# Opening stretch and latents of a two-layer hybrid trunk emitted in hand order, its relative bias on quarters of the PE array

## The chip, the cores and the metric

One core of one Trainium2 chip runs the whole program in one launch. Its engines are TensorE (PE, matmuls; PEld is its weight load), VectorE (DVE), ScalarE (ACT), GpSimd (POOL) and SyncE (SP, which here issues nearly all DMAs). Each takes its instructions from its own queue in order. The metric is device time in microseconds (us), lower is better; a measurement here is the median of several runs, and one more execution is profiled.

## The reference, cut to what matters

Two layers, each with a modulated norm, one wide input projection, three branches (differential attention with a relative position bias, latent attention, a state-space branch), gates, and a feed-forward part; sequence 512, width 1024, all float32. The part that the change touches is the start of layer 0 and the bias, which both layers use:

```python
c_act = jax.nn.silu(c)
mod = c_act @ ada_w[l] + ada_b[l]               # [6 * 1024], here chunks 0 to 3 of 12
sh_m, sc_m, g_m, sh_f, sc_f, g_f = jnp.split(mod[:, None, :], 6, axis=-1)
h = _rmsnorm(x, norm_mix[l]) * (1 + sc_m) + sh_m
proj = h @ w_in[l]                              # the latents are 416 + 16 of its columns
...
dist = qpos[:, :, None] - positions[:, None, :]
bias = jnp.take(rel_table, _t5_bucket(dist), axis=0)   # 32 buckets, 4 heads
```

## The kernel before, in words

Activations are kept as features by tokens: eight tiles of 128 x 512. Matmuls in reduced float32 are made exact enough by splitting each operand into a high and a low part and adding three products (`mm3`, lines 145 to 147). `split` (line 131) makes the parts of a weight: an ACT copy writes `wh`, a DVE subtraction writes `wl`; three buffers of each rotate, each at an offset of some 64-byte lines. A planner orders each engine's queue by its own estimate of when things are ready, except where `tc.manual_schedule` fixes emission order for the engines that it names, or `keep_in_program_order` pins an instruction behind its engine's last one.

The opening prepares layer 0. `conditioning` makes `c_act`. `mod_steps` (line 498 on) loads four chunks of `ada_w` in 512 KB pieces (`wm`, eight buffers) and multiplies them into `macc` on DVE, two multiplies a piece (lines 520 and 522); its last step transposes `macc` on PE and sums it into `mod` (lines 529 to 535). `load_x` (line 485), `transpose_x` (lines 491 and 492) and `norm_r` (line 678; the root by POOL's pow on line 110, spread over partitions on line 685) prepare x. `norm_tiles` (lines 698 to 702) makes, for each half of the tokens and each of eight tiles, `tmp` on DVE, `hh` on ACT and `hl` on DVE.

The relative bias comes in 16 groups (4 blocks of 128 queries, 4 groups of 32 queries in each). A group covers 4 heads by 32 queries, 128 output rows, by the keys that a block sees (128 to 512). Eight steps each compare the key positions with the start of every bucket for 4 queries: `pk <= pq`, as a Sign on ACT (line 653, five of eight), a comparison on DVE (line 655, two) or on POOL (line 649, one). Each comparison tile is then multiplied by a table of bucket differences, high and low part, into all 128 rows of one PSUM bank, 16 matmuls (line 666). The bank is copied to `ob` and written by a POOL DMA to `bias_d` in DRAM, from where the attention reads it much later (line 1294). `START` is the order in which these parts are emitted: L loads x, V loads vectors, T transposes a tile of x, N is a step of the norm, S a step of the modulation, G a bias group.

Then come all norm tiles, `vectors` and `rotary` (small parameters, and sines), and the latents: `latent_product` (line 273 on) multiplies 8 tiles by 432 columns in two halves of 8 steps, 6 matmuls each (lines 299 to 301). After them `mix` begins the state-space branch with `lin_feat` (lines 145 to 147).

Of the kernel before, what the change touches and what calls it, by code (L numbers as in the profile page):

```python
# [9 lines left out]
F32 = mybir.dt.float32  # L10
# [8 lines left out]
P = 128  # L19
# [24 lines left out]
START = "LSSSTGTVNGSNNGSNSGGSGSTTSGTSGSGSGNGGSGTSGSGSGTT"  # L44
# [21 lines left out]
def trunk_kernel(ctx: ExitStack, tc: tile.TileContext, a: dict, out: bass.AP):  # L66
# [206 lines left out]
    def latent_product(l, pool, hh, hl):  # L273
# [12 lines left out]
        def prep():  # L286
            return [group(g) for g in range(3)]
# [210 lines left out]
    def mod_steps(l, j, pool=None):  # L498
# [4 lines left out]
        def step(s):  # L503
            if s == 0:
                acc.append(pool.tile([P, 512], F32, name="macc", bufs=4) if pool else sm.tile([P, 512], F32, name="macc", bufs=2))
# [7 lines left out]
            def pin(ins):  # L513
                tc.keep_in_program_order(ins)
# [11 lines left out]
        def total():  # L526
            mp = mbank()
            for q in range(4):
                ins = nc.tensor.transpose(out=mp[:, q * P:(q + 1) * P], in_=acc[0][:, q * P:(q + 1) * P], identity=ident)
                if pool:  # L530
                    tc.keep_in_program_order(ins)
# [6 lines left out]
        if not pool:  # L538
            return todo + [total]

        def last(s=KT // width - 1):
            step(s)
            total()
        return todo[:-1] + [last]
# [33 lines left out]
    bias_d = dram.tile([DA_H, P, BLK[T]], F32, name="bias_d")  # L578
# [3 lines left out]
    NSIGN = 5  # L582
    early, ahead, SLOW, DEEP = [], [0], (6,), 1
    ORDER = (7, 4, 0, 5, 1, 2, 3, 6)

    W = 2 * P + QG

    def rel_tables(bp):

        pk_i = bp.tile([P, S], I32, name="pk_i")  # L590
        nc.sync.dma_start(out=pk_i, in_=a["positions"].broadcast_to([P, S]))
        tab = bp.tile([P, DA_H], F32, name="tab")
        nc.sync.dma_start(out=tab, in_=a["rel_bias"].unsqueeze(0).broadcast_to([QG, BUCKETS, DA_H]))
        zero = bp.tile([P, 1], F32, name="zero")
        nc.vector.memset(zero, 0.0)
        lr = bp.tile([P, NJ * W], F32R, name="lr")
        nc.scalar.activation(lr, zero.broadcast_to([P, NJ * W]), AF.Copy)

        diff = bp.tile([P, P], F32, name="diff")
        nc.vector.tensor_tensor(out=diff[:, 1:P], in0=ident[:, 1:P], in1=ident[:, 0:P - 1], op=ALU.subtract)  # L600
        nc.vector.tensor_copy(out=diff[:, 0:P:BUCKETS], in_=ident[:, 0:P:BUCKETS])
        hdiff = bp.tile([P, P], F32, name="hdiff")
# [3 lines left out]
        st_row = bp.tile([1, QG, BUCKETS], F32, name="st_row")  # L606
# [4 lines left out]
        start = bp.tile([P, 1], F32, name="start")  # L611
# [15 lines left out]
        delta = bp.tile([P, 2, 2, DA_H], F32R, name="delta")  # L627
        nc.vector.tensor_copy(out=delta[:, :, 0], in_=dv)
        nc.vector.tensor_tensor(out=delta[:, :, 1], in0=dv, in1=delta[:, :, 0], op=ALU.subtract)
        lwv = lr.rearrange("p (j w) -> p j w", w=W)[:, :, 0:2 * P].rearrange("p j (x h q) -> p j x h q", x=2, h=DA_H)  # L630
        for i in range(QG):
            pr = slice(i * BUCKETS, (i + 1) * BUCKETS)
            for kind, js in ((0, slice(0, NSIGN)), (1, slice(NSIGN, NJ))):
                n = js.stop - js.start
                nc.vector.tensor_copy(out=lwv[pr, js, :, :, i],
                                      in_=delta[pr, kind].unsqueeze(1).broadcast_to([BUCKETS, n, 2, DA_H]))
        return pk, pq, pqh, lr[:, 0:NJ * 2 * P].rearrange("p (j x m) -> p j x m", j=NJ, x=2)

    def rel_bias(bp, tables, t, g):

        pk, pq, pqh, lr = tables
        nq = NJ * QG
        n = (t + 1) * P

        def step(t, g, j):
            c, w = (t * 4 + g) * NJ + j, t * P + (P if j == NJ - 1 else g * nq + (j + 1) * QG)
            if j in SLOW:
                st = bp.tile([P, S], F32R, name="sp", bufs=DEEP * len(SLOW) + 1)
                nc.gpsimd.tensor_scalar(out=st[:, 0:w], in0=pk[:, 0:w], scalar1=pq[:, c:c + 1], scalar2=None, op0=ALU.is_le)
            else:  # L650
                st = bp.tile([P, S], F32R, name="st", bufs=7)
                if j < NSIGN:
                    nc.scalar.activation(st[:, 0:w], pk[:, 0:w], AF.Sign, bias=pqh[:, c:c + 1], scale=-1.0)
                else:
                    nc.vector.tensor_scalar(out=st[:, 0:w], in0=pk[:, 0:w], scalar1=pq[:, c:c + 1],
                                            scalar2=None, op0=ALU.is_le)
            return st[:, 0:w]
        bank = mbank()
        while ahead[0] < min(4 * T, 4 * t + g + 1 + DEEP):
            early.append({j: step(ahead[0] // 4, ahead[0] % 4, j) for j in SLOW})  # L660
            ahead[0] += 1
        slow = early.pop(0)
        for j in ORDER:
            st = slow[j] if j in SLOW else step(t, g, j)
            for x in range(2):
                nc.tensor.matmul(bank[:, 0:st.shape[1]], lr[:, j, x], st, start=j == NJ - 1 and x == 0,  # L666
                                 stop=j == ORDER[-1] and x == 1)
        ob = bp.tile([P, S], F32, name="ob", bufs=3)
        nc.any.tensor_copy(out=ob[:, 0:n], in_=bank[:, 0:n])
        nc.gpsimd.dma_start(out=bias_d[:, g * nq:(g + 1) * nq, BLK[t]:BLK[t + 1]], in_=ob[:, 0:n])  # L670


    def norm_r(np_, x_tok):

        ss = small([P, T], "xss", 1)
        for t in range(T):
            sq = np_.tile([P, D], F32, name="sq")
            ins = nc.scalar.activation(sq, x_tok[:, t], AF.Square, accum_out=ss[:, t:t + 1])
            if t == 0:
                tc.keep_in_program_order(ins)  # L680
# [65 lines left out]
    def mix(l, x, hh, hl, ckr, cq, latp, scope):  # L746
# [258 lines left out]
        with ExitStack() as att:  # L1005
# [282 lines left out]
            def da_unit(h, t):  # L1288
# [3 lines left out]
                def scores():  # L1292
                    bt = dap.tile([P, S], F32, name="bt", bufs=3)
                    nc.sync.dma_start(out=bt[:, 0:n], in_=bias_d[h, :, BLK[t]:BLK[t + 1]])
# [200 lines left out]
    norm_scope = ExitStack()  # L1495
    np_ = norm_scope.enter_context(tc.tile_pool(name="norm0", bufs=1, reuse_waits="tile"))
    ip = norm_scope.enter_context(tc.tile_pool(name="init", bufs=1, reuse_waits="tile"))
    bp = norm_scope.enter_context(tc.tile_pool(name="bias", bufs=1, reuse_waits="tile"))
    conditioning(np_)
    tables = rel_tables(bp)  # L1500
    first = [f for j in (0, 2, 1, 3) for f in (mod_steps_pe if j in ON_PE else mod_steps)(0, j, ip)]
    x_tok = ip.tile([P, T, D], F32, name="x_tok")
    xT = big.tile([P, KT, S], F32, name="x16")
    groups = [(t, g) for t in range(T) for g in range(BUCKETS // NJ)]
    turn, rows = transpose_x(x_tok, xT), norm_r(np_, x_tok)
    for what in START:
        if what == "L":
            load_x(x_tok)
        elif what == "V":
            mod_vectors(0, np_)  # L1510
        elif what == "T":
            next(turn)
        elif what == "N":
            rb = next(rows)
        elif what == "S":
            first.pop(0)()
        else:
            rel_bias(bp, tables, *groups.pop(0))
    hh, hl = h_tiles()
    s1 = norm_scale(0, V_NMIX, 8)  # L1520
    for h in range(2):
        norm_tiles(np_, xT, 0, s1, 0, rb, hh, hl, HALF[h], range(KT))
    vectors(0, np_)
    rotary(np_)
    norm_scope.close()
    keep = ctx.enter_context(tc.tile_pool(name="keep", bufs=1, reuse_waits="tile"))
    latp = ctx.enter_context(tc.tile_pool(name="lat", bufs=1, side="right", reuse_waits="tile"))
    ckr = keep.tile([P, T, 176], F32, name="ckr")
    cqs = []
    with tc.tile_pool(name="wx", bufs=1, reuse_waits="tile") as pool:  # L1530
        run_halves(latent_product(0, pool, hh, hl))
# [56 lines left out]
```

## Time and profile before

| | us |
|---|---|
| median of 3 runs (2073.42 to 2077.43) | 2075.08 |
| profiled execution | 2072.72 |
| its span | 2071.0 |
| PE busy | 2043.1 (99%) |
| DVE busy | 1418.6 (68%) |
| ACT busy | 913.8 (44%) |
| POOL busy | 137.1 (7%) |

Matmuls are pipelined, and a busy PE is not a PE at its peak; a busy share is an average over stages with different limits. Times in the rows further down are counted from the start of the span. A duration is that of one instruction; a line with "xN" in an order of time merges N instructions that followed each other, and the mean in a table by line can mix widths ("+ forms").

### The profile page before, as it was taken

The page shows a single profiled execution, that of the slowest core. Times are in us where ns is not written, and L with a number is a line of the kernel's source. Part 1 is how long each engine was busy: PE and PEld are TensorE (multiplying, and loading weights), DVE is VectorE, ACT ScalarE, POOL GpSimd, SP SyncE. Part 2 cuts the span into 40 slices and gives each one's busy share as a digit, 9 for nine tenths or more (in the row PEclk, how much of TensorE's full clock was granted, in tenths as well). Part 3 has the DMA queues.
Part 4 walks back from the last instruction along what each step waited for, and adds up shares of the span by engine and source line. Part 5 has one row for each costly group of instructions (what it writes and reads, how often), then busy time and mean ns, then how long its engine had stood idle before and what let it go on. Part 6 is the DMA issues. An engine that isn't in the chain of part 4 may idle for free.

```text
span 2071.0 us, 30143 instructions
## 1 busy us (share of the span) xinstructions
PE 2043.1 (99%) x11469; PEld 1769.7 (85%) x11469; DVE 1418.6 (68%) x2742; ACT 913.8 (44%) x1683; POOL 137.1 (7%) x162
## 2 busy tenths in 40 slices
PE   8999999999999999999999999999999999999999
PEld 7888987789888988888898888888998898888888
DVE  7788887756876678658757888775566566553553
ACT  6744445535533454224434544454444335432441
POOL 4200011002100000000000000110020000000000
PEclk8999999999999999999999999999999999999999
DMA  8523232233445255655443223212333243323222
GB/s 268 150 69 85 78 116 90 87 108 113 152 153 169 94 187 165 196 179 166 153 141 85 79 62 89 64 48 79 93 93 93 92 133 92 102 92 102 92 92 82
DMA packets 224542, 237.20 MB, mean 115 GB/s; under 512 B 16126, under 2 KB 195742, under 8 KB 224142
## 3 DMA queue, kind: packets, MB, share of 16 engines
q1 hardware_dynamic: 221646, 232.63, 36.3%
q0 software_dynamic: 2752, 2.65, 0.5%
q8 instruction: 90, 1.47, 0.3%
q14 instruction: 54, 0.44, 0.1%
HBM read 226.30 MB, written 8.91 MB: 114 GB/s over the span
## 4 chain that ended last, share of the span: by engine, by line
PE 87%; DVE 7%; DMA 2%; POOL 2%; issue 2%; ACT 1%; SPq 0%; POOLq 0%; DVEq 0%; ACTq 0%
PE mb L145 22%; PE mb L147 21%; PE mb L146 21%; PE mb L224 3%; PE mb L226 3%; PE mb L225 3%; PE ab L965 1%; DVE wl L141 1%; PE mb L666 1%; PE ab L1140 1%; PE ab L1177 1%; DVE macc L522 1%; PE ab L1326 1%; PE ab L1082 1%; POOL r_r L110 1%
## 5 line engine op out<-in xcount | busy, mean ns | idle before, releaser
L145 PE MATMUL mb<-hh,wh 128*128 128x512 f32 (+1 forms) x1376 | 538.2, 392 | 1.8 <-DVE g L778 0.9
L147 PE MATMUL mb<-hh,wl 128*128 128x512 f32 (+1 forms) x1376 | 532.4, 387 | 0.0
L146 PE MATMUL mb<-hl,wh 128*128 128x512 f32 (+1 forms) x1376 | 531.3, 386 | 0.0
L141 DVE TENSOR_TENSOR wl<-wr,wh 128x1024 fp32r<-128x1024 f32 (+2 forms) x312 | 374.9, 1203 | 193.8 <-ACT wh L140 192.5
L140 ACT ACTIVATE wh<-wr 128x1024 fp32r<-128x1024 f32 (+2 forms) x312 | 324.7, 1042 | 338.4 <-PE mb L146 260.5
L147 PEld LDWEIGHTS mb<-hh,wl 128*128 128x128 f32 x1376 | 258.4, 188 | 51.7
L145 PEld LDWEIGHTS mb<-hh,wh 128*128 128x128 f32 x1376 | 258.3, 188 | 51.8 <-DVE g L778 1.8
L146 PEld LDWEIGHTS mb<-hl,wh 128*128 128x128 f32 x1376 | 258.8, 188 | 49.1 <-DVE hl L702 1.2
L1423 DVE SCALAR_TENSOR_TENSOR fu<-mb,vec,fu 128x510 f32<-128x510 f32 (+1 forms) x176 | 129.8, 745 | 90.5 <-ACT fu L1421 88.9
L224 PE MATMUL mb<-wh,hh 128*128 128x256 f32 x640 | 180.1, 281 | 0.0
L226 PE MATMUL mb<-wh,hl 128*128 128x256 f32 x640 | 178.6, 279 | 0.0
L225 PE MATMUL mb<-wl,hh 128*128 128x256 f32 x640 | 178.5, 279 | 0.0
L145 PE MATMUL mb<-gh,wh 128*128 128x512 f32 (+1 forms) x432 | 151.2, 350 | 0.0
L147 PE MATMUL mb<-gh,wl 128*128 128x512 f32 (+1 forms) x432 | 150.6, 349 | 0.0
L146 PE MATMUL mb<-gl,wh 128*128 128x512 f32 (+1 forms) x432 | 150.5, 348 | 0.0
L1421 ACT ACTIVATE fu<-mb,vec 128x512 f32<-128x512 f32 x88 | 67.9, 774 | 149.7 <-PE mb L147 149.7
L224 PEld LDWEIGHTS mb<-wh,hh 128*128 128x128 f32 x640 | 120.0, 188 | 1.2 <-ACT wh L140 0.4
L225 PEld LDWEIGHTS mb<-wl,hh 128*128 128x128 f32 x640 | 120.1, 188 | 0.4
L226 PEld LDWEIGHTS mb<-wh,hl 128*128 128x128 f32 x640 | 120.2, 188 | 0.0
L522 DVE SCALAR_TENSOR_TENSOR macc<-wg,c_act,macc 128x512 f32<-128x512 f32 x140 | 104.6, 747 | 20.0 <-DMA wg<-in_ada_w_dram 19.2
L145 PE MATMUL mb<-yh,wh 128*128 128x512 f32 x256 | 104.5, 408 | 0.9 <-ACT g L769 0.9
L147 PE MATMUL mb<-yh,wl 128*128 128x512 f32 x256 | 100.3, 392 | 0.0
(333 smaller groups left out, 3373.9 us busy)
## 6 DMA issues: line engine op xcount, KB each, us to landing
wr<-in_w_in_dram SPq DMA_DIRECT2D x88, 512.0 KB
wr<-in_ffn_w_up_dram SPq DMA_DIRECT2D x88, 512.0 KB
wg<-in_ada_w_dram SPq DMA_DIRECT2D x160, 256.0 KB
wr<-in_ffn_w_down_dram SPq DMA_DIRECT2D x40, 512.0 KB
wr<-in_w_in_dram SPq DMA_DIRECT2D x64, 256.0 KB
wm<-in_ada_w_dram SPq DMA_DIRECT2D x16, 512.0 KB
wr<-in_w_branch_c_dram SPq DMA_DIRECT2D x16, 512.0 KB
wr<-in_w_out_dram SPq DMA_DIRECT2D x16, 512.0 KB
```

What stands on the lines that cost most here:

```text
L110: nc.gpsimd.tensor_tensor(out=r, in0=ms, in1=nhalf[:, 0:1].broadcast_to([P, n]), op=ALU.pow)
L140: nc.scalar.activation(hi, raw[:, 0:n], AF.Copy)
L141: nc.vector.tensor_tensor(out=lo, in0=raw[:, 0:n], in1=hi, op=ALU.subtract)
L145: nc.tensor.matmul(o, lh, rh, start=first, stop=False)
L146: nc.tensor.matmul(o, lh, rl, start=False, stop=False)
L147: nc.tensor.matmul(o, ll, rh, start=False, stop=last)
L224: nc.tensor.matmul(o, hh[:, kk, ts_], wh[:, sl], start=first and k == 0, stop=False)
L225: nc.tensor.matmul(o, hh[:, kk, ts_], wl[:, sl], start=False, stop=False)
L226: nc.tensor.matmul(o, hl[:, kk, ts_], wh[:, sl], start=False, stop=last and k == 3)
L522: ins = nc.vector.scalar_tensor_tensor(out=acc[0], in0=rk, scalar=c_act[:, kk:kk + 1], in1=acc[0], op0=ALU.mult, op1=ALU.add)
L1421: nc.scalar.activation(u, bank, AF.Identity, bias=v[:, V_FCB + ti:V_FCB + ti + 1], scale=tap(2))
L1423: nc.vector.scalar_tensor_tensor(out=u[:, s_:], in0=bank[:, 0:S - s_], scalar=tap(2 - s_), in1=u[:, s_:], op0=ALU.mult, op1=ALU.add)
```

## The change

The whole opening up to the end of the latents now stands in one region whose order is that of emission, on every engine. What is emitted outside the region may still be placed among it by the planner. `START` has new letters: M is the sum of a modulation chunk, no longer tied to its last step; G is now only the comparisons of a bias group, g its matmuls, copy and write. In the opening stand four groups, those of 512 keys; the other twelve stand in the latents, by `BESIDE`, one entry for each of the 16 steps, together with `vectors` (V) and `rotary` (R). A tile of norm is emitted just ahead of the latents that read it: those of the first half between the weight splits, those of the second half after each step of the first.

A bias group's comparison tiles and table are float32, with no high and low part, and each of the eight steps has its own 32 output rows: steps 2i and 2i + 1 add into quarter i of the array's columns, the odd one starting the sum. So a group is 8 matmuls with 32 columns of weights. POOL compares two of eight steps; the late groups have four Signs and two DVE comparisons, the early ones six Signs. All copies of transposed x are ACT's. The tiles `wh` and `wl` have names and buffers of their own, with other offsets. `bias_d` has queries ahead of heads.

```diff
-START = "LSSSTGTVNGSNNGSNSGGSGSTTSGTSGSGSGNGGSGTSGSGSGTT"
+START = "SSSLSVSMGSTTNSSSMgGTTNSSTTNSSMTTNgGSNSgGSMg"
+BESIDE = ("", "G", "", "Gg", "", "Gg", "", "Gg",
+          "Gg", "Gg", "Gg", "Gg", "VGg", "RGg", "Gg", "Gg")
...
-            i = -uses[0] % 3
+            i = uses[0] % 3
             uses[0] += 1
-            at = ((i + shift) % 4, (i + 3 + shift) % 4)
-            hi, lo = [wp.tile([P, 1024 + 3 * LINE], F32R, name=nm)[:, LINE * o:LINE * o + n] for nm, o in zip(("wh", "wl"), at)]
+            hi, lo = [wp.tile([P, 1024 + 3 * LINE], F32R, name=f"{nm}{i}", bufs=1)[:, LINE * o:LINE * o + n]
+                      for nm, o in (("wh", (2 * i + shift) % 4), ("wl", (2 * i + 1 + shift) % 4))]
...
-            nc.any.tensor_copy(out=xT[:, k], in_=xp)
+            nc.scalar.activation(xT[:, k], xp, AF.Copy)
...
+    ORDER = (1, 3, 5, 7, 0, 2, 4, 6)
...
+    def bias_steps(bp, tables, t, g, late):
+
+        pk, pq, pqh, _ = tables
+        out = []
+        for j in ORDER:
+            c, w = (t * 4 + g) * NJ + j, t * P + (P if j % 2 else g * NJ * QG + (j + 1) * QG)
+            st = bp.tile([P, S], F32, name="st", bufs=12)[:, 0:w]
+            sign = j not in ((3, 4, 6, 7) if late else (4, 6))
+            if sign:
+                nc.scalar.activation(st, pk[:, 0:w], AF.Sign, bias=pqh[:, c:c + 1], scale=-1.0)
             else:
...
+                eng = nc.gpsimd if j in (4, 6) else nc.vector
+                eng.tensor_scalar(out=st, in0=pk[:, 0:w], scalar1=pq[:, c:c + 1], scalar2=None, op0=ALU.is_le)
+            out.append((j, st, sign))
+        return out
+
+    def bias_sum(bp, tables, t, g, steps_, late):
+
+        n, nq = (t + 1) * P, NJ * QG
+        bank = abank() if late else mbank()
+        for j, st, sign in steps_:
+            own = slice(j // 2 * NC, (j // 2 + 1) * NC)
+            nc.tensor.matmul(bank[own, 0:st.shape[1]], tables[3][:, 0 if sign else 1, j % 2], st,
+                             start=j % 2 == 1, stop=j % 2 == 0, tile_position=(0, own.start))
         ob = bp.tile([P, S], F32, name="ob", bufs=3)
+        if late:
+            nc.vector.tensor_copy(out=ob[:, 0:n], in_=bank[:, 0:n])
+        else:
+            nc.scalar.activation(ob[:, 0:n], bank[:, 0:n], AF.Copy)
+        nc.gpsimd.dma_start(out=bias_d[g * nq:(g + 1) * nq].rearrange("q h n -> (q h) n")[:, BLK[t]:BLK[t + 1]], in_=ob[:, 0:n])
...
+    with tc.manual_schedule(engines=None):
+        conditioning(np_)
+        tables = rel_tables(bp, ip)
+        first = [mod_steps(0, j, ip) for j in (0, 2, 1, 3)]
+        totals, first = [f.pop() for f in first], [s_ for f in first for s_ in f]
...
+        def scaled(h, ks):
+            norm_tiles(np_, xT, 0, s1, 0, rb, hh, hl, HALF[h], ks)
+        with tc.tile_pool(name="wx", bufs=1, reuse_waits="tile") as pool:
+            prep, mm = latent_product(0, pool, hh, hl)
+            weights = prep(lambda g: scaled(0, range(2 * g, 2 * g + 2)))
+            scaled(0, range(6, KT))
+            for h in range(2):
+                for k, _ in enumerate(mm(weights, h)):
+                    if h == 0:
+                        scaled(1, range(k, k + 1))
+                    for what in BESIDE[h * KT + k]:
+                        if what == "V":
+                            vectors(0, np_)
+                        elif what == "R":
+                            rotary(np_)
+                        else:
+                            do(what, True)
+            while groups or turned:
+                do("G", True)
+                do("g", True)
```

## Rows read from the trace of the kernel before

**Rows 1.** Table of stretches: busy us (instructions) of each engine, granted clock, DMA share, GB/s.

```profile
0.00:91.30 91.30, 79.38 (x419) 73.26 (x420) 72.55 (x212) 62.59 (x134) 33.96 (x56) 0.93 0.72 228
...
0.00:30.00 30.00, 22.26 (x124) 20.73 (x125) 21.70 (x98) 18.13 (x45) 9.76 (x34) 0.96 0.94 333
```

**Rows 2.** Order of time, PE, end of the latents: start, us, engine, line, out<-in.

```profile
86.22 0.36 PE L301 MATMUL mb<-wh,hl 128*128 128x432 f32 x1
...
91.09 0.36 PE L301 MATMUL mb<-wh,hl 128*128 128x432 f32 x1
...
91.29 0.40 PE L145 MATMUL mb<-hh,wh 128*128 128x512 f32 x1
```

**Rows 3.** Order of time, all engines, around the latents' start.

```profile
68.14 0.16 DVE L535 TENSOR_TENSOR mod<-modsum,vec 128x4 f32<-128x4 f32 x1
...
68.53 1.26 DVE L698 SCALAR_TENSOR_TENSOR tmp<-x,s,ab 128x256 f32<-128x256 f32 x3
...
70.46 0.44 PE L299 MATMUL mb<-wh,hh 128*128 128x432 f32 x1
```

**Rows 4.** Order of time, PE, float32 products of full width (1082) and of halves (1177).

```profile
290.58 1.46 PE L1082 MATMUL ab<-wm,lat 128*128 128x192 f32 x8
...
291.88 1.03 PE L1104 MATMUL ab<-wm,lat 128*128 128x256 f32 x4
...
328.11 0.66 PE L1177 MATMUL ab<-pT,vv 128*64 128x128 f32 x8
...
335.37 0.88 PE L1177 MATMUL ab<-pT,vv 128*64 128x128 f32 x12
```

**Rows 5.** Order of time, all engines, near the start.

```profile
4.90 0.43 DVE L614 CAST pk<-pk_i 128x512 f32<-128x512 int32 x1 [2.85 <-DMA pk_i<-in_positions_dram]
```

**Rows 6.** Chain that ended last, pieces in order of time: start, us, what.

```profile
3.87 6.67 DMA x_tok<-in_x_dram
```

**Rows 7.** Durations by line up to 90 us: busy us, mean ns, idle before.

```profile
L522 DVE SCALAR_TENSOR_TENSOR macc<-wm,c_act,macc 128x512 f32<-128x512 f32 x28 | 21.3, 760 | 0.2
...
L534 DVE TENSOR_REDUCE modsum<-mb 128x4 f32<-128x512 f32 x4 | 2.7, 684 | 2.3 <-PE mb L529 2.2
...
L141 DVE TENSOR_TENSOR wl<-wr,wh 128x864 fp32r<-128x864 f32 (+1 forms) x6 | 6.5, 1094 | 0.0
...
L701 ACT ACTIVATE hh<-tmp,mod 128x256 fp32r<-128x256 f32 x16 | 7.3, 501 | 5.4 <-DVE tmp L698 5.4
...
L702 DVE SCALAR_TENSOR_TENSOR hl<-tmp,mod,hh 128x256 fp32r<-128x256 f32 x16 | 7.2, 487 | 2.6 <-ACT hh L701 2.6
...
L698 DVE SCALAR_TENSOR_TENSOR tmp<-x,s,ab 128x256 f32<-128x256 f32 x16 | 6.8, 472 | 0.0
...
L678 ACT ACTIVATE sq<-x_tok 128x1024 f32<-128x1024 f32 x4 | 4.2, 1040 | 0.0
...
L492 ACT COPY x<-ab 128x512 f32<-128x512 f32 x3 | 1.8, 589 | 2.9 <-PE ab L491 2.9
```

**Rows 8.** The same by form up to 72 us, one engine at a time: Sign, and comparisons.

```profile
L653 ACT ACTIVATE st<-pk,pqh 128x500 fp32r<-128x500 f32 x1 | 0.7, 699 | 0.0
...
L649 POOL TENSOR_SCALAR sp<-pk,pq 128x508 fp32r<-128x508 f32 x1 | 2.2, 2248 | 0.2 <-PE mb L666 0.2
...
L649 POOL TENSOR_SCALAR sp<-pk,pq 128x252 fp32r<-128x252 f32 x1 | 0.9, 914 | 1.8 <-PE mb L666 1.8
...
L655 DVE TENSOR_SCALAR st<-pk,pq 128x512 fp32r<-128x512 f32 x4 | 2.0, 495 | 0.0
```

**Rows 9.** Order of time, PE, feed-forward: every 24th matmul, that is every weight buffer.

```profile
1901.32 0.39 PE L145 MATMUL mb<-hh,wh 128*128 128x512 f32 x1
...
1906.76 0.39 PE L145 MATMUL mb<-hh,wh 128*128 128x512 f32 x1
...
1912.20 0.39 PE L145 MATMUL mb<-hh,wh 128*128 128x512 f32 x1
```

**Rows 10.** Order of time, DVE and POOL beside each other.

```profile
55.81 1.28 DVE L655 TENSOR_SCALAR st<-pk,pq 128x408 fp32r<-128x408 f32 x1
...
55.88 1.61 POOL L649 TENSOR_SCALAR sp<-pk,pq 128x444 fp32r<-128x444 f32 x1
```

More of the change, by code (lines that the diff above doesn't have):

```diff
@@ L284, in group, with prep @@
             return split(raw, 2 * width, pool if g == 3 else None, 1, 0 if l else LINE)
-        def prep():
-            return [group(g) for g in range(3)]
+        def prep(between=None):
+            out = []
+            for g in range(3):
+                out.append(group(g))
+                if between:
+                    between(g)
+            return out
         def mm(weights, h):
@@ L504, in step @@
             if s == 0:
-                acc.append(pool.tile([P, 512], F32, name="macc", bufs=4) if pool else sm.tile([P, 512], F32, name="macc", bufs=2))
+                acc.append(pool.tile([P, 512], F32, name="macc", bufs=3) if pool else sm.tile([P, 512], F32, name="macc", bufs=2))
             src = a["ada_w"][l][s * width * P:(s + 1) * width * P, j * 512:(j + 1) * 512].rearrange("(k p) c -> p k c", p=P)
@@ L513, in pin @@
             def pin(ins):
-                tc.keep_in_program_order(ins)
+                if not pool:
+                    tc.keep_in_program_order(ins)
             for k in range(width):
@@ L528, in total @@
             for q in range(4):
-                ins = nc.tensor.transpose(out=mp[:, q * P:(q + 1) * P], in_=acc[0][:, q * P:(q + 1) * P], identity=ident)
-                if pool:
-                    tc.keep_in_program_order(ins)
+                nc.tensor.transpose(out=mp[:, q * P:(q + 1) * P], in_=acc[0][:, q * P:(q + 1) * P], identity=ident)
             cs_ = slice(4 * j, 4 * j + 4)
@@ L537, in mod_steps @@
         todo = [lambda s=s: step(s) for s in range(KT // width)]
[L538 to L544, printed above, removed]
+        return todo + [total]
     def mod_steps_pe(l, j, pool):
@@ L575, in mod_queue @@
         return out + [late]
-    bias_d = dram.tile([DA_H, P, BLK[T]], F32, name="bias_d")
+    bias_d = dram.tile([P, DA_H, BLK[T]], F32, name="bias_d")
     x_d = dram.tile([P, KT, S], F32, name="x_d")
@@ L610, in rel_tables @@
         nc.tensor.matmul(stp[:, 0:1], st_row.rearrange("o i b -> o (i b)"), ones[0:1, 0:1], start=True, stop=True)
-        start = bp.tile([P, 1], F32, name="start")
+        start = ip.tile([P, 1], F32, name="start")
         nc.vector.tensor_copy(out=start, in_=stp[:, 0:1])
@@ L637, in rel_tables @@
[L637 to L649, printed above, removed]
-            else:
[L651 to L667, printed above, removed]
-        ob = bp.tile([P, S], F32, name="ob", bufs=3)
-        nc.any.tensor_copy(out=ob[:, 0:n], in_=bank[:, 0:n])
-        nc.gpsimd.dma_start(out=bias_d[:, g * nq:(g + 1) * nq, BLK[t]:BLK[t + 1]], in_=ob[:, 0:n])
@@ new lines, in rel_tables @@
+            for odd in range(2):
+                nc.vector.tensor_copy(out=lr[pr, :, odd, odd, i], in_=dv[pr])
+        return pk, pq, pqh, lr.rearrange("p k j i q h -> p k j (i q h)")
+    GROUPS = [(t, g) for t in range(T)[::-1] for g in range(4)]
+    def bias_steps(bp, tables, t, g, late):
+        pk, pq, pqh, _ = tables
+        out = []
+        for j in ORDER:
[4 more added lines that the diff above has]
+                nc.scalar.activation(st, pk[:, 0:w], AF.Sign, bias=pqh[:, c:c + 1], scale=-1.0)
+            else:
+                eng = nc.gpsimd if j in (4, 6) else nc.vector
+                eng.tensor_scalar(out=st, in0=pk[:, 0:w], scalar1=pq[:, c:c + 1], scalar2=None, op0=ALU.is_le)
+            out.append((j, st, sign))
+        return out
@@ L1293, in scores @@
                     bt = dap.tile([P, S], F32, name="bt", bufs=3)
-                    nc.sync.dma_start(out=bt[:, 0:n], in_=bias_d[h, :, BLK[t]:BLK[t + 1]])
+                    nc.sync.dma_start(out=bt[:, 0:n], in_=bias_d[:, h, BLK[t]:BLK[t + 1]])
                     nc.gpsimd.affine_select(bt[:, n - P:n], bt[:, n - P:n], pattern=[[-1, P]], compare_op=ALU.is_ge,
@@ L1492, in finish @@
                 nc.sync.dma_start(out=ov[:, 2:4, (KT - 2) * P:], in_=ot[:, 2:4, (KT - 2) * P:])
-    norm_scope = ExitStack()
+    keep = ctx.enter_context(tc.tile_pool(name="keep", bufs=1, reuse_waits="tile"))
+    norm_scope, init_scope, bias_scope = ExitStack(), ExitStack(), ExitStack()
+    bp = bias_scope.enter_context(tc.tile_pool(name="bias", bufs=1, reuse_waits="tile"))
     np_ = norm_scope.enter_context(tc.tile_pool(name="norm0", bufs=1, reuse_waits="tile"))
-    ip = norm_scope.enter_context(tc.tile_pool(name="init", bufs=1, reuse_waits="tile"))
@@ L1498, in trunk_kernel @@
[L1498 to L1502, printed above, removed]
-    xT = big.tile([P, KT, S], F32, name="x16")
[L1504 to L1531, printed above, removed]
+    ip = init_scope.enter_context(tc.tile_pool(name="init", bufs=1, reuse_waits="tile"))
@@ new lines, in trunk_kernel, with do @@
+    xT = big.tile([P, KT, S], F32, name="x16")
+    groups, turned, cqs = list(GROUPS), [], []
+    with tc.manual_schedule(engines=None):
[3 more added lines that the diff above has]
+        totals, first = [f.pop() for f in first], [s_ for f in first for s_ in f]
+        x_tok = ip.tile([P, T, D], F32, name="x_tok")
+        turn, rows = transpose_x(x_tok, xT), norm_r(np_, x_tok)
+        def do(what, late=False):
+            if what == "G" and groups:
+                t, g = groups.pop(0)
+                turned.append((t, g, bias_steps(bp, tables, t, g, late)))
+            elif what == "g" and turned:
+                bias_sum(bp, tables, *turned.pop(0), late)
+        for what in START:
+            if what == "L":
+                load_x(x_tok)
+            elif what == "V":
+                mod_vectors(0, np_)
+            elif what == "T":
+                next(turn)
+            elif what == "N":
+                rb = next(rows)
+            elif what == "S":
+                first.pop(0)()
+            elif what == "M":
+                totals.pop(0)()
+            else:
+                do(what)
+        init_scope.close()
+        latp = ctx.enter_context(tc.tile_pool(name="lat", bufs=1, side="right", reuse_waits="tile"))
+        ckr = keep.tile([P, T, 176], F32, name="ckr")
+        hh, hl = h_tiles()
+        s1 = norm_scale(0, V_NMIX, 8)
+        def scaled(h, ks):
[13 more added lines that the diff above has]
+                            rotary(np_)
+                        else:
+                            do(what, True)
+            while groups or turned:
+                do("G", True)
+                do("g", True)
+        norm_scope.close()
@@ L1532, in trunk_kernel @@
+    bias_scope.close()
     for l in range(DEPTH):
```

35 lines of the change are left out of this document (10 added, 25 removed).

## The prediction

> **What bounds the kernel now.** I read the page's busy shares first (the table above), then a table of stretches, then the order of time around the end of the opening, then durations by line. TensorE (PE) is busy for 99% of the span. A share says nothing of a stage, so stretches come next: up to 91.3 us no engine is full. PE holds 79.4 us of pipelined matmuls there, VectorE (DVE) 72.6, ScalarE (ACT) 62.6, GpSimd (POOL) 34.0 [rows 1]. At 91.29 the SSM branch's first projection starts on line 145 [rows 2], and from there PE streams products to the end. So a change of the opening is worth how much earlier or later PE gets to that work. The order of time shows what held it: the last modulation sum is added at 68.14 (line 535), the latents' first matmul follows at 70.46 [rows 3], and their last stands just before 91.29. The latents wait for the DVE's modulation multiplies, which the planner had spread among sixteen bias groups.
>
> The profiled execution took 2072.72 us, 1.72 more than its span; the median of three runs is 2.36 higher. I work against 2072.72 and add 2.36 at the end.
>
> **What goes from PE.** A bias group was 16 full-array matmuls, 256 in all. Now it is 8 float32 ones of 32 columns, each issued as two instructions, as float32 products are now (line 1082: 8 instructions for 4 products). Those 8, 192 columns each, step by (291.88 - 290.58)/8 = 0.1625, or 0.85 ns a column, which is 0.108 for 128 columns. Line 1177 uses halves of the array: 12 instructions of 128 columns take 0.88 and 8 take 0.66, so 0.055 a step [rows 4]. Halves overlap twofold; I take quarters as fourfold with 0.055 as the least step: 16 steps make 1.7 us at 512 columns, 1.3 at 384, 0.9 at 256 and 128. The other end is twofold: 3.5, 2.6, 1.7, 0.9. I take the first, and add 0.2 a group for entering and leaving. The Trainium skill, "TensorE: Matmul & The Clock Gate", section "Measured speedup vs the span model", gives three column tiles as 2.38 times one, not 3; by that the twelve late groups would need some 3 us more. No row here has quarters.
>
> PE gets cheaper, but the opening doesn't wait for PE. The question is what queues in emission order do to DVE and ACT.
>
> **Opening, up to the latents' first split.** DVE: 32 memsets, the tables, pq, pqh and the table copies end at about 9.7, since pk waits until 4.90 for its positions [rows 5] and all of that is queued about it. Then 28 multiplies of 0.760 and the four first ones of chunks, taken as 0.5 like a 512-column comparison: 23.3 [rows 7, 8]. Four sums of 0.684 with their small adds 3.4, the vectors 0.5. The fourth weight load now stands behind four x loads: 8 x 0.524 MB at the first stretch's 333 GB/s, from 3.87 [rows 1, 6], is 16.5, where the multiplies would want it at 14.0: 2.5. DVE alone would be done at 39, far ahead of 68.14.
>
> ACT is later. In emission order the first bias product, g1, stands on PE behind the second sum, which needs multiply step 8: 9.7 + 11.6 + 0.5 + 0.9 + 2.5 = 25.2; transposes 0.6 and g1 2.0 make 27.8. Behind that wait stands the rest of ACT's opening: four bias evictions (0.59 each, like x's), three groups of six Sign activations (four near 0.70, two somewhat shorter: 4.0), six x evictions of 0.589 (all eight are ACT's now, three were), three squares of 1.040 and 0.19 [rows 7, 8]: 2.4 + 12.0 + 3.5 + 3.7 = 21.6, to 49.4. On top, g3 and g4 end about 1 us each after their last Sign; and the rstd's pow stands on POOL behind two comparisons of the third group (up to 2.2 each [rows 8], twice as many as before), and PE's broadcast of it stands before g3: 2.5. So 54, between 49 and 58.
>
> **Norm tiles, in emission order.** Each of 16 half tiles is tmp (DVE, 0.472), hh (ACT, 0.501), hl (DVE, 0.487) [rows 7]. The planner ran three tmp in a row, 1.26 [rows 3], with hh beside. Now hl stands behind its own hh on DVE, and the next tmp behind hl, so a tile costs the chain: 1.46, of which DVE waits 0.5. From 54: the first split, ACT then DVE, 2.0; 16 x 1.46 = 23.4; three more splits at 1.09 and 0.5 of waiting, 4.8; four bias groups with two DVE comparisons each (under 0.495), 3.7; three bias evictions 1.7. Sum 35.6: the last half tile is ready at 89.6. PE has then done the first half's latents, three late groups between them.
>
> **What PE still owes.** Eight steps of 6 latent matmuls at (91.09 - 86.22)/25 = 0.195 [rows 2]: 9.4. Nine groups, one of 384 columns at 1.5 and eight at 1.1: 10.3. Two transposes of vectors 0.5. Together 20.2, so PE has done at 109.8 what it had done at 91.3: 18.5 later.
>
> Two costs lie outside. `vectors` is emitted inside the late groups: r3's memset comes late on DVE, ten loads on SP wait for it, and PE's transpose, DVE's copy and all groups and latents behind them wait for the landing: about 5 us, with `rotary`'s chain between DVE and ACT behind. POOL paces the last groups near that time too (0.914 a comparison at 252 columns [rows 8], two of them and a DMA issue a group). The other way, what is emitted behind the region may be placed into its gaps: line 145 can fill PE from about 75, when the second half's first tiles are ready, as far as its weights are split. I set these equal, 6 us each.
>
> **Edits at nothing.** The offsets of wh and wl: on lines 145 to 147 24 matmuls take 5.44 with one buffer and the next [rows 9]; nothing, within 3 us either way. bias_d's layout: the same 16 writes and row lengths, read only hundreds of microseconds later, which covers them. macc with three buffers: the fourth chunk takes the first's, summed long before. The SSM weights and x_d load beside the late groups, and the 109.8 already takes them as there; without that cover, line 145 waits some us more.
>
> Sum: 2072.7 + 18.5 = 2091.2, plus 2.4: 2093.
>
> **Rivals.**
> A, faster: PE's own work decides, because ACT doesn't lag DVE in the opening and the tiles keep ahead. Latents would start 3.5 after DVE's 39, at 43, and PE would owe 16 x 1.17 + 4 x 1.5 + 8 x 1.1 + 0.5 = 34: line 145 at 77, 14 earlier, 2061. For it: the sums come some 29 us earlier. Against: the tile chain of 1.46 (with splits 2.2) against PE's 1.17 a step, and the late g1. It decides if the first latent matmul comes before 57 and PE doesn't wait after it. Chance 0.20, over 2053 to 2070.
> B, slower still: POOL's sixteen added comparisons block DVE. A DVE comparison of 408 columns at 55.81 took 1.28 beside one of POOL [rows 10], where 512 columns take 0.495 [rows 8]: 0.8 lost, 16 times 13 us, 2106. Against: the multiplies' mean of 0.760 holds beside POOL. [...] Chance 0.12; if nothing fills the gaps, the time is the same.
> C, no change: ACT's end is 47 and the gaps are filled for all but a third of the remaining 11 us: within 4 us of 2075. Chance 0.08.
>
> **How the numbers follow.** The forecast has 0.60 and its own range, 2081 to 2104 (opening 49 to 58, gaps 6 us filled or not). The bound of "same" is 0.2%, 4 us, about what a measurement of this kernel can tell. Slower: 0.60 + 0.12, less 0.01 of the forecast's low end: 0.71. Faster: A and 0.02 of C, 0.22. Same 0.07. The range of 8 in 10 goes from 2060, leaving half of A out, to 2106, leaving half of B out.
>
> **What would show it.** In the changed profile: Sign activations of the second group not before 26; the first latent matmul near 57; DVE idle about 0.5 before each hl on line 702's successor; line 145 dense only after 100; late groups' steps near 0.06 us. The forecast is wrong if line 145 is dense before 91, if bias evictions begin before 20, if tiles overlap as before, or if 24 matmuls of lines 145 to 147 no longer take 5.44.

## The result and the profile after

The changed kernel took 2099.83 us (median of 4 runs, 2099.49 to 2100.26) against 2074.25 for the kernel before beside it: ratio 1.0123, 95% interval 1.0106 to 1.0141, so 25.5 us slower (ratios below are turned into us with 2075). The forecast was 2093 in a range of 2060 to 2106. Its direction and mechanism held; the size came out 7 us short.

Line numbers move: `mm3` is now on 147 to 149, `split` on 142 and 143, the latents on 306 to 308, Signs on 641, comparisons on 644, the bias products on 654, `tmp`, `hh`, `hl` on 687, 690, 691. The table of stretches of the changed kernel, columns as in [rows 1]:

```profile
0.00:91.30 91.30, 45.41 (x236) 27.09 (x236) 57.95 (x152) 45.61 (x84) 27.98 (x30) 0.85 0.56 201
...
91.30:130.00 38.70, 35.41 (x248) 24.50 (x247) 21.56 (x60) 21.47 (x51) 18.02 (x42) 0.96 0.37 105
```

Against [rows 1] every engine did less by 91.3: PE 45.4 instead of 79.4, DVE 58.0 instead of 72.6, ACT 45.6 instead of 62.6. PE's part is partly cheaper products; DVE's and ACT's is work that came late. The order of time shows where. First ACT (start, us, engine, line, and in brackets the idle time before and what ended it):

```profile
7.42 3.58 ACT L641 ACTIVATE st<-pk,pqh 128x512 f32<-128x512 f32 x6 [4.39 <-DVE pqh L616]
20.08 0.60 ACT L499 ACTIVATE x<-ab 128x512 f32<-128x512 f32 x1 [9.08 <-PE ab L498]
...
28.98 0.60 ACT L660 ACTIVATE ob<-mb 128x512 f32<-128x512 f32 x1 [6.42 <-PE mb L654]
29.48 3.62 ACT L641 ACTIVATE st<-pk,pqh 128x512 f32<-128x512 f32 x6
...
49.65 0.60 ACT L660 ACTIVATE ob<-mb 128x512 f32<-128x512 f32 x1 [6.47 <-PE mb L654]
50.14 3.73 ACT L641 ACTIVATE st<-pk,pqh 128x512 f32<-128x512 f32 x6
55.44 0.60 ACT L660 ACTIVATE ob<-mb 128x512 f32<-128x512 f32 x1 [1.57 <-PE mb L654]
55.93 0.91 ACT L142 ACTIVATE wh<-wr 128x864 fp32r<-128x864 f32 x1
```

ACT stands idle at the head of its own queue: 9.08 for the first x transposes, 6.42 for the first bias sum, 6.47 for the third. The second group's Signs start at 29.48, queued behind an eviction, although the first four need nothing from PE: there are twelve comparison buffers, and the first group has taken eight. The third sum is late for another reason: PE's broadcast at 45.03 stands ahead of it and waits 8.51 for the pow on POOL, which starts at 43.93, behind that group's two comparisons (from 40.56). PE, from the first bias sum to the end of the late groups:

```profile
26.25 2.62 PE L654 MATMUL mb<-st,lr 128*32 128x512 f32 x16
...
45.03 2.07 PE L674 MATMUL ab<-ident,nh_r 128*128 128x128 f32 x8 [8.51 <-POOL nh_r L112]
...
58.92 0.73 PE L306 MATMUL mb<-wh,hh 128*128 128x432 f32 x1 [3.52 <-ACT hh L690]
...
76.80 3.11 PE L654 MATMUL ab<-st,lr 128*32 128x384 f32 x16 [10.43 <-ACT st L641]
...
83.66 1.38 PE L654 MATMUL ab<-st,lr 128*32 128x384 f32 x16
...
94.12 0.91 PE L654 MATMUL ab<-st,lr 128*32 128x256 f32 x16
...
101.47 0.27 PE L417 MATMUL ab<-ident,r 126*128 126x126 f32 x1
...
109.12 0.23 PE L418 MATMUL ab<-ident,r 82*128 82x82 f32 x1
...
120.14 1.15 PE L654 MATMUL ab<-st,lr 128*32 128x128 f32 x16 [2.91 <-ACT st L641]
...
123.68 0.58 PE L654 MATMUL ab<-st,lr 128*32 128x128 f32 x16
```

The latents start at 58.92, 11.5 before [rows 3]; then PE waits 10.43 for the Signs of the first late group, queued on ACT behind ten norm tiles. A norm tile on DVE, and what DVE waited for between 44 and 92 (us in total, times, longest):

```profile
88.44 0.47 DVE L687 SCALAR_TENSOR_TENSOR tmp<-x,s,ab 128x256 f32<-128x256 f32 x1
89.49 0.48 DVE L691 SCALAR_TENSOR_TENSOR hl<-tmp,mod,hh 128x256 fp32r<-128x256 f32 x1 [0.58 <-ACT hh L690]
```

```profile
DVE hl L691 <- ACT hh L690: 9.3, 16, 0.7
DVE modsum L540 <- PE mb L537: 7.6, 1, 7.6
DVE wl L143 <- ACT wh L142: 5.6, 3, 4.9
```

Every one of the sixteen `hl` waits for its `hh`. Nearly all of the loss arises here. A mark for it is the first product of line 954 (965 before), in the state-space branch: every kernel of this document has 675 instructions of PE ahead of it, the same ones but for the form of the bias products. It comes at 161.0 instead of 135.8, 25.2 later, of 26.6 by which the two profiled spans differ. In the feed-forward nothing changed; every 24th matmul still steps by 5.44, as in [rows 9]:

```profile
1925.85 0.39 PE L147 MATMUL mb<-hh,wh 128*128 128x512 f32 x1
...
1931.29 0.39 PE L147 MATMUL mb<-hh,wh 128*128 128x512 f32 x1
...
1936.73 0.39 PE L147 MATMUL mb<-hh,wh 128*128 128x512 f32 x1
```

### The profile page after: what moved, and what is told of

Same layout as the page of the kernel before. It is cut to its first block, busy times and chain, and to the rows that moved or that the text cites. A ratio compares the mean times of both kernels' runs of the same rounds, so it can differ in the third digit from the quotient of the medians.

```text
span 2097.6 us, 30057 instructions
## 1 busy us (share of the span) xinstructions
PE 2030.6 (97%) x11469; PEld 1736.2 (83%) x11469; DVE 1418.3 (68%) x2731; ACT 912.3 (43%) x1675; POOL 149.8 (7%) x178
## 4 chain that ended last, share of the span: by engine, by line
PE 85%; DVE 8%; ACT 2%; POOL 2%; issue 2%; DMA 2%; SPq 0%; POOLq 0%; DVEq 0%; ACTq 0%
PE mb L147 21%; PE mb L149 21%; PE mb L148 21%; PE mb L226 3%; PE mb L228 3%; PE mb L227 3%; DVE wl L143 1%; PE ab L954 1%; PE ab L1129 1%; PE ab L1166 1%; DVE macc L530 1%; PE ab L654 1%; DMA wg<-in_ada_w_dram 1%; PE ab L1315 1%; PE ab L1071 1%
## 5 line engine op out<-in xcount | busy, mean ns | idle before, releaser
L530 DVE SCALAR_TENSOR_TENSOR macc<-wg,c_act,macc 128x512 f32<-128x512 f32 x140 | 104.7, 748 | 21.6 <-DMA wg<-in_ada_w_dram 20.5
```

The costliest lines, as they stand in the source:

```text
L530: ins = nc.vector.scalar_tensor_tensor(out=acc[0], in0=rk, scalar=c_act[:, kk:kk + 1], in1=acc[0], op0=ALU.mult, op1=ALU.add)
```

## The experiments

Theory: the loss is ACT and DVE standing in emission order behind waits that the planner would have filled. Rivals: PE's quarter products or its clock; POOL's added comparisons. Each kernel is the changed one with the edit shown. Summary (us against before, by the ratio; first latent matmul and first product of line 954 from the order of time). The kernel before had a median of 2076.16 beside e1 to e4, of 2074.66 beside e5 to e8 and of 2074.16 beside e9 to e12, so experiments of different groups compare to some 2 us:

| kernel | median us | ratio [95%] | us | first latent | line 954 |
|---|---|---|---|---|---|
| before (profiled) | | 1 | 0 | 70.5 | 135.8 |
| changed | 2099.83 | 1.0123 [1.0106, 1.0141] | +25.5 | 58.9 | 161.0 |
| e1_planner | 2077.17 | 1.0006 [0.9997, 1.0016] | +1 | 46.6 | 138.8 |
| e2_start | 2085.47 | 1.0040 [1.0025, 1.0055] | +8 | 46.4 | 148.2 |
| e3_pairs | 2094.25 | 1.0083 [1.0068, 1.0098] | +17 | 60.3 | 156.5 |
| e4_vec | 2102.40 | 1.0123 [1.0107, 1.0138] | +25.5 | 64.3 | 164.0 |
| e5_pe_only | 2075.63 | 1.0005 [0.9995, 1.0014] | +1 | 47.8 | 138.5 |
| e6_all_hand | 2078.89 | 1.0018 [1.0008, 1.0027] | +4 | 47.7 | 141.1 |
| e7_pe_start | 2072.68 | 0.9983 [0.9973, 0.9993] | -3.5 | 46.3 | 134.3 |
| e8_pinned | 2076.45 | 1.0011 [1.0001, 1.0020] | +2 | 45.6 | 137.9 |
| e9_pool | 2100.27 | 1.0126 [1.0110, 1.0141] | +26 | 58.2 | 162.5 |
| e10_twos | 2072.18 | 0.9989 [0.9980, 0.9998] | -2.3 | 45.0 | 132.7 |
| e11_pe_act | 2084.30 | 1.0050 [1.0032, 1.0068] | +10 | 53.7 | 145.8 |
| e12_pe_dve | 2087.60 | 1.0065 [1.0050, 1.0080] | +13.5 | 48.2 | 149.1 |

**Who is ordered by hand.** Five kernels differ only in the set of engines that the region fixes: none (e1), PE (e5), PE and ACT (e11), PE and DVE (e12), all (the change).

```diff
-    with tc.manual_schedule(engines=None):
+    with ExitStack():                                                        # e1
+    with tc.manual_schedule(engines={mybir.EngineType.PE}):                   # e5
+    with tc.manual_schedule(engines={mybir.EngineType.PE, mybir.EngineType.Activation}):    # e11
+    with tc.manual_schedule(engines={mybir.EngineType.PE, mybir.EngineType.DVE}):           # e12
```

> The changed kernel without the hand-ordered region: the planner orders the queues again; quarters, twelve late groups, two comparisons a group on POOL and everything else stay. Theory (the loss is the order: ACT and DVE stand behind waits in emission order): most of the loss goes, line 147 dense before 95 us, time 2065 to 2083. Rival 1 (the quarters cost PE more than the full-array groups did, or keep its clock low): stays over 2092. Rival 2 (POOL's added comparisons block DVE): they are still there, stays over 2088.

> The changed kernel with its region fixing emission order on PE alone; ACT, DVE, POOL and SP are ordered by the planner again. Theory (the loss is ACT's and DVE's emission order): ACT and DVE no longer stand behind g1 and the norm tiles as before, PE still waits for g1 behind the second sum; first latent at 48 to 55, time 2077 to 2090. Rival (PE's own hand order loses it): 2094 to 2100.

> The changed kernel with emission order on PE and ACT; DVE, POOL and SP ordered by the planner. Theory of the prediction (ACT, standing behind the first bias sum, is what comes late; the tile chain is DVE's): most of the loss returns, first latent at 54 to 60, time 2088 to 2097. Rival (DVE's order makes the loss: the sums and the hl of each tile): first latent before 52, time 2076 to 2084.

> The same with emission order on PE and DVE; ACT, POOL and SP ordered by the planner. Theory: ACT free, but each hl still stands behind its hh and the fourth sum behind PE: 2079 to 2087. Rival (DVE's order makes the loss): 2090 to 2100.

e1 and e5 give the whole loss back, with the quarters, the late groups and POOL's comparisons still in. So the loss is in the order, and not in PE's, and both rivals fall as its cause. e11 keeps 9 us over e5 and e12 keeps 12.5: neither engine alone, as both pairs of expectations had it, but both. They lose at different places. With ACT in order the first latent comes at 53.68, with DVE in order at 48.18, near e5's 47.79; the rest of the way to 58.92 comes only with all engines in order. But with DVE in order each tile is again a chain, and the late group waits for a DVE comparison behind ten of them. DVE's waits from 44 to 92 in e5, then in e12, and PE in e12:

```profile
DVE ob L658 <- PE ab L654: 7.9, 8, 2.4
...
DVE hl L691 <- ACT hh L690: 1.2, 1, 1.2
```

```profile
DVE hl L691 <- ACT hh L690: 10.7, 16, 1.7
DVE ob L658 <- PE ab L654: 2.8, 3, 1.1
```

```profile
65.18 2.76 PE L654 MATMUL ab<-st,lr 128*32 128x384 f32 x14 [9.18 <-DVE st L644]
```

In e5 one `hl` waits for its `hh`, 1.2 us; the planner sets other tiles' work between the two. The two single parts make 21.5 of 24.5 us; the remaining 3 (POOL's and SP's order, or the two engines together) were not separated.

**START.** Only the order of the opening:

```diff
-START = "SSSLSVSMGSTTNSSSMgGTTNSSTTNSSMTTNgGSNSgGSMg"
+START = "VSSSLSGgSGgSMGSSTTgTTSSMNNTTSSNNTTNSSMGSSgM"
```

> START alone reordered: vectors loaded first, each of three bias sums right behind its comparisons and ahead of the x transposes, squares before the fourth group, so that ACT stands behind no late modulation sum. Theory: first latent matmul at 41 to 47 instead of 58.9, some of the 12 to 18 given back by the tile chain and the wait of vectors: 2082 to 2092. Rival 1 (PE's clock or quarters): the first latent comes early too, but PE needs as much longer for the rest: 2095 to 2100. Rival 2 (POOL blocks DVE): DVE's multiplies and sums aren't done earlier, first latent not before 54, 2094 to 2100.

The latents came 12.5 earlier, and 17 us came back by the ratio, 14 by the medians: within the theory's time, and neither rival's. What stayed is seen on PE, which stands at the same place as in the changed kernel for the same 10.44:

```profile
46.44 0.47 PE L306 MATMUL mb<-wh,hh 128*128 128x432 f32 x1 [3.26 <-ACT hh L690]
...
64.19 3.11 PE L654 MATMUL ab<-st,lr 128*32 128x384 f32 x16 [10.44 <-ACT st L641]
```

**Tiles in pairs.**

```diff
...
-                    if h == 0:
-                        scaled(1, range(k, k + 1))
+                    if h == 0 and k % 2 == 0:
+                        scaled(1, range(k, k + 2))   # scaled(): all tmp, then all hh, then all hl
```

> Norm tiles emitted in pairs (tmp, tmp, hh, hh, hl, hl) instead of one by one, in both halves; nothing else. Theory (the chain of 1.46 us a tile paces PE): a pair takes about 2.0 instead of 2.9, the last half tile comes 5 to 7 us earlier than 89.97, time 2092 to 2096. Rival 1 (PE's own work paces): the tiles come earlier, PE doesn't, 2098 to 2101.

DVE of e3, two pairs:

```profile
65.69 0.87 DVE L1530 SCALAR_TENSOR_TENSOR tmp<-x,s,ab 128x256 f32<-128x256 f32 x2
66.74 0.88 DVE L1536 SCALAR_TENSOR_TENSOR hl<-tmp,mod,hh 128x256 fp32r<-128x256 f32 x2 [0.19 <-ACT hh L1534]
67.54 0.87 DVE L1530 SCALAR_TENSOR_TENSOR tmp<-x,s,ab 128x256 f32<-128x256 f32 x2
68.59 0.88 DVE L1536 SCALAR_TENSOR_TENSOR hl<-tmp,mod,hh 128x256 fp32r<-128x256 f32 x2 [0.19 <-ACT hh L1534]
```

A pair takes 1.85 instead of 2 x 1.45, DVE waits 1.6 us for all `hh` together, the last `hl` ends at 83.6 instead of 90.0, and the time falls by 5.6 us by the medians, 8 by the ratios: the chain of a tile did pace PE.

**All engines by hand, but better.** START of e2, pairs of e3, and the fifth group's comparisons emitted at the end of START:

```diff
-BESIDE = ("", "G", "", "Gg", ...
+BESIDE = ("", "", "", "Gg", ...      # START ends in "...SSgMG"
```

> All engines in emission order: START of e2_start, norm tiles in pairs as in e3_pairs, and the fifth group's comparisons at the end of START instead of behind ten norm tiles. Theory (waits in emission order, each of its own place): e2_start gave 14, pairs 6, and the 10.4 us that PE stood idle for the fifth group go in part: 2070 to 2080. Rival (ACT's and DVE's work as such bounds the stretch, so the gains don't add): 2080 to 2086.

2078.89: the theory's range. PE's wait for the first late group is gone, one of 4.03 for the second stays (at 62.04). Three edits of emission order recover 22 of 25.5 us without the planner.

**Loads of `vectors` and `rotary` early.**

```diff
+        small_parts = {"V": vector_parts(0, np_), "R": rotary_parts(np_)}
+        for part in small_parts.values():
+            next(part)                # loads and memsets only; the rest stays in BESIDE
         init_scope.close()
```

> The loads (and memsets) of vectors and rotary issued at the end of the opening, their arithmetic left where it is. Theory: PE's transposes of vectors and DVE's copy no longer stand behind a landing at 106.9; PE's products of line 147 filled that wait, so only part comes back: 2 to 5 us, 2095 to 2098. Rival (that wait is filled in full): 2099 to 2101.

No gain, and by the medians 2.6 us more, outside both forecasts. The edit does remove the wait: the two transposes follow each other. The loads, however, now stand on SP ahead of the latents' weights, and they wait themselves: for 13.3 us, until 52.09, SP stands behind a memset that DVE reaches only after the fourth modulation sum (51.90). The weights that were loaded from 25.59 on in the changed kernel now follow at 56.38, ACT waits 4.7 for `wr`, and the first latent comes at 64.25 instead of 58.92:

```profile
64.25 0.73 PE L306 MATMUL mb<-wh,hh 128*128 128x432 f32 x1 [8.30 <-ACT hh L700]
...
106.45 0.27 PE L424 MATMUL ab<-ident,r 126*128 126x126 f32 x1
106.56 0.23 PE L425 MATMUL ab<-ident,r 82*128 82x82 f32 x1
```

It started 5.3 later and reached line 954 3.0 later, so about 2 were won between; as a test of that wait by itself it is spoilt by its own loads.

**POOL's second comparison.**

```diff
-                eng = nc.gpsimd if j in (4, 6) else nc.vector
+                eng = nc.gpsimd if j == 6 else nc.vector
```

> The changed kernel with one of POOL's two comparisons a group (step 4) given to DVE, one left on POOL as before the change. Rival B of the prediction (POOL's added comparisons block DVE for 0.8 us each): 8 to 13 us less than the changed kernel, 2087 to 2092. Theory (the waits in emission order set the time): within 3 us of it, 2097 to 2103.

2100.27, the same as the changed kernel, as the theory had it. But the edit hardly changes what DVE spends, so by itself it doesn't decide on rival B. DVE and POOL of the changed kernel, then of e9, at about the same group:

```profile
84.81 1.30 DVE L644 TENSOR_SCALAR st<-pk,pq 128x384 f32<-128x384 f32 x2
...
84.69 2.43 POOL L644 TENSOR_SCALAR st<-pk,pq 128x340 f32<-128x340 f32 x2 [1.81 <-PE ab L654]
```

```profile
84.04 1.25 DVE L644 TENSOR_SCALAR st<-pk,pq 128x384 f32<-128x384 f32 x3
...
83.30 1.15 POOL L644 TENSOR_SCALAR st<-pk,pq 128x348 f32<-128x348 f32 x1 [1.25 <-PE ab L654]
```

Two DVE comparisons beside two of POOL take as long as three beside one. The blocking is real (at 76.68 in the changed kernel, with POOL idle until 78.89, the pair took 0.74, so 0.56 less than here), and what the edit saves is spent by the third comparison. What decides on rival B is e1 and e5, and the size: added over the changed kernel's first 130 us, DVE's instructions took 4.4 us longer beside a comparison of POOL than the same ones alone, 1.9 of it in the comparisons, where the rival needed 13.

**Quarters between whole-array products.** The changed kernel runs a group's eight products in a row, as sixteen instructions. In e1 the planner runs them as soon as their comparisons are there:

```profile
51.11 0.36 PE L308 MATMUL mb<-wh,hl 128*128 128x432 f32 x1
51.40 0.83 PE L654 MATMUL ab<-st,lr 128*32 128x384 f32 x2
52.16 0.46 PE L306 MATMUL mb<-wh,hh 128*128 128x432 f32 x1
52.46 0.36 PE L307 MATMUL mb<-wl,hh 128*128 128x432 f32 x1
...
62.42 0.84 PE L654 MATMUL ab<-st,lr 128*32 128x384 f32 x4
63.19 0.46 PE L308 MATMUL mb<-wh,hl 128*128 128x432 f32 x1
```

The two instructions at 51.40 are one float32 product, both on the same quarter, and take 0.76 to the next latent. The four at 62.42 are two products on two quarters and take 0.77: the second costs nothing. So a product that stands alone is paid in full, while a group of eight in a row took 1.32 (83.66 to 84.98). The latents on both sides step by 0.29 and 0.30 instead of 0.195. That is due to the quarters and not to the change from reduced to full float32: in the kernel before, on the whole array, that change takes 0.233 at 290.35 where line 147 otherwise steps by 0.227, and the way back 0.447 at 294.69 where the two steps alone make 0.443. e8 was to mend that:

```diff
+            if x:
+                tc.keep_in_program_order(ins)      # the 16 instructions of a group, in e1's kernel
```

> The planner's order of e1_planner, but each group's 16 quarter products pinned to stand one behind the other. In e1_planner PE ran them two, four or eight at a time between latents, 21.2 us for the twelve late groups, where the changed kernel's uninterrupted sixteen take 1.38, 0.91 and 0.58 at full clock. Theory (quarters overlap only when products of all four stand in a row): 5 to 10 us less than e1_planner, 2067 to 2073. Rival (those gaps were waiting time anyway, DVE and ACT set the pace): 2075 to 2081.

The edit did not do what it meant to: the pin holds the order of the sixteen and still lets latents in between, and PE runs them in the same twos, fours and eights. It says nothing of either reading. e7 and e10 put PE in hand order with e2's START, e10 with the late sums in twos and sixteen comparison buffers for them:

```diff
+    with tc.manual_schedule(engines={mybir.EngineType.PE}):      # e7 and e10, START of e2
...
+BESIDE = ("G", "", "G", "", "", "ggGG", "", "", "ggGG", "", "ggGG", "V", "ggGG", "R", "ggGG", "")   # e10
```

> Emission order fixed on PE alone, and START as in e2_start. Theory: both lags gone, first latent at 40 to 47, PE waits little after it: 2063 to 2077. Rival (PE's hand order behind the first latent, the first late group ahead of half of the latents, still waits 10 us as in e2_start): 2078 to 2086.

> e7_pe_start with the late groups' sums two at a time, six places for PE to change between whole array and quarters instead of twelve and more, and sixteen comparison buffers of their own for them. Theory (PE loses 0.2 us at each change and some 5 us inside groups that wait for their last comparisons): 3 to 8 us below e7_pe_start, 2065 to 2070. Rival (DVE, ACT and POOL deliver no faster, so PE waits as long at fewer places): 2070 to 2076.

e7 came out at 2072.68, below before by 1.5 to 5.6 us by the interval; e10 adds nothing that can be told from it, so its rival stands. In e10 a group that waits for POOL still breaks up, and the planner lets state-space products in:

```profile
86.63 0.33 PE L654 MATMUL ab<-st,lr 128*32 128x84 f32 x2 [0.64 <-POOL st L644]
87.12 0.35 PE L654 MATMUL ab<-st,lr 128*32 128x92 f32 x2 [0.16 <-POOL st L644]
87.83 0.41 PE L654 MATMUL ab<-st,lr 128*32 128x128 f32 x4
```

Why do e1 and e5 only draw level, with latents 23 us earlier than before? Before, the sixteen groups ran while PE had little else to do; twelve of them now stand where PE is full. In e5, 22.7 ahead at the first latent and 2.7 behind at line 954, PE lost 25.3 us between. The late groups' steps between 53.75 and 95.93 add up to 22.2 of them, 4.1 spent waiting inside the groups. The latents took 22.4 where they took 20.8 before (70.46 to 91.29), and the state-space products beside and behind them 23.1 where they took 21.8: together 25.1.

## Why the prediction was right, and where it was short

- **ACT stands behind the first bias sum: right.** The sum was forecast done at 27.8, it ended at 28.87; the second group's Signs not before 26, they began at 29.48; ACT's end at 54, the first split began at 55.93; the first latent near 57, it came at 58.92. That the end is so near is in part luck. From 28.98 on ACT worked 18.9 us in place of 21.6, since its instructions follow each other more closely than they last (an eviction of 0.60 is followed after 0.50). It stood idle for 8.0 in place of 4.5, most of it in the wait behind POOL's pow. e11 against e5 shows the cause: ACT's order alone moves the first latent from 47.8 to 53.7.
- **The tile chain of 1.46 with 0.5 of waiting on DVE: right.** The period is 1.45, the wait 0.58, the last half tile ends at 89.97 where 89.6 stood (2 later at the start, 34.0 from the first split in place of 35.6). e3 and e12 confirm that it costs time. That it holds the first late group's comparisons back as well, 10.43 us on PE, was in the sum only as part of the 35.6.
- **Late groups' steps near 0.06 us: right in time at 384 and 256 columns, by two errors that cancel.** Where no wait stood inside, 16 steps took 1.32 and 1.37 at 384 columns, 0.83 to 0.99 at 256 and, in e5, 0.51 at 128, where 1.3, 0.9 and 0.9 stood. But only every second product has all the columns (`w` in the diff): in the group at 83.66 the others have 292 to 316. All columns of a group one after the other at 0.85 ns [rows 4] would take 3.5 times as long as measured at 384, 3.2 to 3.4 times at 256 and 2.7 times at 128, not four times. The forecast had full width in every step and a fourfold overlap; at 128 its least step of 0.055 was not the least (0.51 for sixteen is 0.032). The Trainium skill, "TensorE: Matmul & The Clock Gate", section "Measured speedup vs the span model", gives 2.38 for three column tiles, which is 0.79 of threefold. No row here has three; the four show 0.81 to 0.89 of fourfold at 256 and 384 columns, so the overlap is about the page's, but the 3 us more did not come, since the columns were fewer. The 0.2 a group for entering and leaving was right too: a tenth on each side.
- **What PE still owed, 20.2 us from the last half tile: the term that was too small, by some 6 us.** PE ran its last late group to 127.6 and had by then put in 53 state-space products, 12.1 us at 0.228 (87 of them take 19.86 in e5): 115.5 in place of 109.8, 24.2 behind [rows 2] in place of 18.5. From 90.27 on the forecast has 42 latents at 0.195, 8.2; nine groups, 8.5, and 1.8 for entering and leaving them; and 0.5. The groups took 10.6, since some waited inside for comparisons (2.48 at 90.27, 1.61 at 98.59). The latents with the changes took 10.5 in place of 10.0: six between two groups step 1.37, but the last six took 2.46. The changes beside the state-space products cost another 1.0. And the wait of `rotary`, set equal to what fills it, was not filled: ACT's Signs stand behind its sines, and PE is idle for 2.91 ahead of 120.14. Behind it, as behind the 10.43, the granted clock is at the lower of its two levels, 1.2 GHz, and latents step by 0.36 (stretches, columns as above):

```profile
76.80:79.80 3.00, 3.00 (x16) 1.54 (x16) 1.89 (x5) 2.06 (x5) 0.91 (x1) 0.50 0.05 15
...
79.80:82.50 2.70, 2.70 (x8) 2.48 (x8) 2.43 (x5) 2.08 (x6) 1.40 (x3) 0.50 0.00 0
83.00:90.00 7.00, 7.00 (x54) 4.42 (x52) 5.27 (x13) 4.55 (x11) 4.41 (x5) 1.00 0.15 59
...
120.20:123.60 3.40, 3.40 (x22) 2.51 (x22) 1.41 (x5) 2.08 (x8) 2.11 (x4) 0.50 0.62 193
```

- **`vectors` and fillers set equal: right for `vectors`.** Line 147 put 33 products into the 7.62 us between its two transposes.
- **Behind the region** little more was lost. Line 954 starts 25.2 late at 161.0, and from there to the end PE has the same 10,794 instructions in the same order in both kernels. The last attention product is 26.6 late at 1618.2; most of these 1.4 us come in two stretches, near 585 and 814, ahead of line 147. What made them stays open.
- **Edits at nothing: right where seen.** 24 matmuls still take 5.44, and the 1.4 us behind line 954 bound what the new offsets and the bias layout cost there. They were not tested one by one.
- **Rival A** fell by its own sign: the first latent came at 58.92, not before 57, and PE waited after it. It had a true half: the opening need not wait for ACT (46.3 in e7). Its other half fell: it had PE owe 34 us from there, and in e7 the last late group ended at 92.9 with 14 state-space products put in, 43 us. **Rival B** fell with e1 and e5 and by the 4.4 us above; and it could not be sixteen times, since the four early groups have no comparison on DVE.

## What to carry to other kernels

Where one order is fixed by hand for all engines, a short instruction behind a long wait sets the time: fix it for the bottleneck engine alone, or write the order so that no engine's queue goes to another engine and back within one tile (pairs, comparisons ahead of the tiles that need nothing of them). Work moved from a stretch where the bottleneck engine is idle to one where it is full must be paid there in full, whatever its new price. A load moved early takes along the wait for its own buffer, and the loads that were next stand behind both (e4).

## What was not expected of the hardware

Quarter products overlap when products of different quarters stand in a row: eight of them, sixteen instructions of 384 and fewer columns, took 1.32 us, 3.5 times less than one after the other. One product alone takes 0.76, and two on two quarters 0.77. Going from the whole array to quarters and back cost PE about 0.2 us, a tenth on each side (six latents 1.37 instead of 1.17). The first late group, behind 10.43 us of waiting, took 3.04 to the next latent instead of 1.32, at a granted clock of 0.50, which alone would make it 2.64. DVE and POOL slow each other only in part: two DVE comparisons that took 0.74 alone took 1.30 inside two of POOL's, which lasted 2.43, so neither engine waited for the other's whole instruction.
